# Two transformer blocks on one core: the first block's up-projections by seven products

## The chip, the cores and the metric

The kernel runs on one core of one Trainium2 chip. The metric is the time of one execution on the device in microseconds (us), as the median of several runs. The core has five engines that take instructions of their own queues in order: TensorE (PE in the rows, PEld for its weight loads), the vector engine VectorE (DVE), ScalarE (ACT), GpSimd (POOL) and SyncE (SP), which here mostly issues transfers. An instruction waits until what it needs has been signalled by the others.

## The reference

Two blocks of two layers each work on x, 512 tokens of 1024 features in fp32. What the change touches is the feed-forward step of the first block:

```
up = h2 @ w_up[l]                       # 1024 x 5632
a, v = up[..., :D_FF], up[..., D_FF:]   # D_FF = 2816
a = causal_depthwise_conv(a, conv_w[l], conv_b[l])   # width 3, over tokens
x = x + (jax.nn.gelu(a, approximate=False) * v) @ w_down[l]
```

with h2 the normed x. The second block's feed-forward step is `silu(g) * u` on the same sizes, without the convolution. In front of each stands the block's attention, and between the blocks a norm.

## The kernel before

Features lie on the 128 partitions and tokens along a row, so a tile of x is 128x512. Every fp32 product is three products of a split operand: a value is hi (rounded by ScalarE, L132) plus lo (the rest, by VectorE, L133), and `mm3` computes hi·hi, hi·lo and lo·hi. Weights come as raw tiles of 512 KB (128x1024 fp32; six buffers) on SyncE's queue, in an order that a plan fixes ahead; `_emit` splits the next one into one of four pairs of hi and lo buffers (`put`), and `pump` lets it do so once TensorE's work on an earlier one is issued. A raw buffer is loaded anew once its split has read it. All engines work through their instructions in the order in which the program issues them.

The feed-forward step (`ffn`) goes by groups of 128 of the 2816 columns, 22 in all, in four parts: 6, 6, 4 and 6 groups (`FPARTS`). A part computes the up-projection of its groups, two at a time (a pair), then the down-projection: units of two groups by 512 output columns ("fd", 24 matmuls of 512 columns each), which add to x (L660). Behind the first such unit stands what is left of the part's last pair, and behind a part of four groups also the first product of the next part (`started`).

A pair is computed in one of two ways; `PLAIN` gives for each block the group from which the second is used. Plain: `pair` for "fa" and "fv", 96 matmuls of 512 columns; then ScalarE and VectorE do the convolution of a (L1081 to L1083), ScalarE the Gelu (L1084), VectorE the product with v (L1152) and the split of the result (L237, L238: acth and actl). By seven products (`spair`): the 1024 x 256 weights of a pair and the activations are halved both ways into 2x2 blocks, and seven products of sums of blocks (24 matmuls of 256 columns each) take the place of eight. Products of the same sum of activations need sums of weight blocks, which VectorE makes (L327, `sum0`, `sum1`, `sum2`, `post5`: four for each pair); the sums of activations are made once for each layer (`factors`). The parts of a result are put together from three accumulators A, D and B by copies on ScalarE (s1, p5, d) and steps on VectorE (L1110 to L1125). Before, the first block has PLAIN 22 (all plain) and the second 6 (groups 6 to 21, so eight pairs in each layer: three, two and three in the last three parts).

In the first block the memory of the later cross attention is normed in the background (`mem_norm`, `mem_split`) while the second layer's feed-forward step runs.

Of the kernel before, what the change touches and what calls it, by code (L numbers as in the profile page):

```python
# [4 lines left out]
F32 = mybir.dt.float32  # L5
# [5 lines left out]
MUL, ADD, SUB, MAX = ALU.mult, ALU.add, ALU.subtract, ALU.max  # L11
P = 128
S = 512
D = 1024
# [300 lines left out]
    return chunk(name, raws, [unit(r["kc"], nc_, split, (i,)) for i, r in enumerate(raws)])  # L315


def schunks(name, w, c1, c2):


    b = [block(w, r, 4, c, 256) for r, c in ((0, c1), (0, c2), (512, c2), (512, c1))]

    b11, b12, b22, b21 = b
    box = {}

    def add(c, to, x, y):
        c.nc.vector.tensor_tensor(to, x, y, op=ADD)  # L327

    def sum0(c, r):

        box["t"] = c.pf.tile([P, 1024], F32, tag="t0", bufs=1, name=c.nm("t0")).rearrange("p (k c) -> p k c", k=4)
        add(c, box["t"], r[0], r[1])

    def sum1(c, r):

        add(c, r[0], r[0], r[1])

    def sum2(c, r):

        add(c, r[0], r[0], r[1])  # L340

    def post5(c, r):

        add(c, r[0], r[0], r[1])

    def temp(c, hi, lo, raws):
        c.put(hi, lo, box.pop("t"))


    u = [dict(unit(4, 256, whole, (b11,), 0), pre=sum0, praws=(b11, b12)),  # L350
         dict(unit(4, 256, temp, (b11,), 0), pre=sum1, praws=(b12, b22)),
         dict(unit(4, 256, whole, (b11,), 0), pre=sum2, praws=(b11, b12)),
         unit(4, 256, whole, (b22,), 1),
         dict(unit(4, 256, whole, (b21, b11), 1, 1), post=post5, praws=(b21, b11)),
         unit(4, 256, whole, (b12,), 1),
         unit(4, 256, whole, (b21,), 1)]
    out = [chunk(name, [], [x]) for x in u]
    out[0]["raws"] = b
    return out
# [77 lines left out]
FPARTS = ((0, 6), (6, 12), (12, 16), (16, 22))  # L437
FPARTS_END = ((0, 6), (6, 12), (12, 18), (18, 22))

PLAIN = (22, 6)  # L440


def ffn_plan(wu, wd, b, end=False):
    pl, late, first = [], [], []
    pairs = {f: schunks("fs", wu, 2816 + 128 * f, 128 * f) for f in range(PLAIN[b], 22, 2)}
    parts = FPARTS_END if end else FPARTS
    for f0, f1 in parts:
        for f in range(f0, f1, 2):
            if f < PLAIN[b]:
                pl.append(wchunk("fa", wu, 0, 8, 128 * f))  # L450
                pl.append(wchunk("fv", wu, 0, 8, 2816 + 128 * f))
                continue

            c = pairs[f]
            if not first:
                pl += c[:1] + late
            pl += c[1:6]
            late, first = c[6:], []
        if end and f1 == 22:
            pl += late  # L460
            for i in range(4):
                pl.append(wchunk("fd", wd, 128 * f0, f1 - f0, 256 * i))
            continue
        for i in range(2):
            for f in range(f0, f1, 2):
                pl.append(chunk("fd", [block(wd, 128 * f, 2, 512 * i, 512)], [unit(2, 512)]))
                if i == 0 and f == f0:
                    pl += late
                    late = []
                    if f1 - f0 == 4 and f1 >= PLAIN[b]:  # L470
                        first = pairs[f1][:1]
                        pl += first
    return pl


class Kern(Ctx):
# [515 lines left out]
                yield  # L992


    def factors(self):


        nc = self.nc
# [18 lines left out]
        for j in range(5):  # L1017
            cur = None
            if j < 4:
                xa, xb = self.t("xa"), self.t("xb")  # L1020
                for t, k in ((xa, j), (xb, j + 4)):
                    nc.vector.scalar_tensor_tensor(t, self.x[k], self.ngain(k), self.Rb, op0=MUL, op1=MUL)
                a11, a21, a12, a22 = xa[:, H[0]], xa[:, H[1]], xb[:, H[0]], xb[:, H[1]]
                s14, s23 = self.t("s14"), self.t("s23")
                tt(s14[:, H[0]], a22, a21, op=SUB)
                tt(s23[:, H[0]], a11, s14[:, H[0]], op=ADD)
                tt(s23[:, H[1]], a21, a11, op=SUB)
                tt(s14[:, H[1]], s23[:, H[0]], a12, op=SUB)
                cur = a11, xb, s14, s23
                yield  # L1030
            if last:
                a11, xb, s14, s23 = last
                if j % 2:
                    two = self.ft("Ah"), self.ft("Al")
                put(a11, ("11",), tiles=two, at=256 * ((j - 1) % 2))
                put(s14, ("1", "4"))
                put(s23, ("2", "3"), scale=-1.0)
                rest.append(xb)
            last = cur
            yield  # L1040
# [28 lines left out]
    def ffn(self, l, after, conv):  # L1069
# [22 lines left out]
        def spair(f, ah, al):  # L1092

            A, D, B = (self.ps() for _ in range(3))
            half = lambda t, nt: t[:, H[nt]]
            self.product(A, "11", True)
            yield
            s1 = self.t("s1")
            nc.scalar.copy(s1, A)
            self.product(D, "1", True)  # L1100
            self.settle()
            p5 = self.t("p5")
            nc.scalar.copy(p5, D)
            self.product(A, "2", False)
            a = [self.t("a") for _ in range(2)]
            self.product(D, "4", False)
            d = self.t("d")
            nc.scalar.copy(d, D)
            for nt in range(2):
                nc.vector.scalar_tensor_tensor(a[nt][:, H[0]], half(A, nt), -1.0, half(d, nt), op0=MUL, op1=SUB)  # L1110
            self.finish(gf)
# [27 lines left out]
        for i, (f0, f1) in enumerate(parts):  # L1139
            end = f1 == 22  # L1140
            ah, al = lists[i]
            for f in range(f0, f1, 2):
                if f < plain:
# [12 lines left out]
                    if f == 0:  # L1156
                        self.first_pair(self.next("fa"), ev_a, self.norm_gen())
                        if plain < 22:
                            gf = self.bg(self.factors())
                    else:  # L1160
                        self.pair("fa", ev_a)
                    self.pair("fv", ev_v)
# [17 lines left out]
            for c in range(2):  # L1180
# [18 lines left out]
                for u in range(0, n, 2):  # L1199
# [12 lines left out]
                    if u == 0 and c == 0:  # L1212
                        if last is not None:

                            end_of(last)
                            last = None
                        if end:
                            after[0]()
                            self.A = None
                        if n == 4 and f1 >= plain:  # L1220
                            started = spair(f1, *lists[i + 1])
                            next(started)
                        self.settle()


    def mem_norm(self):
# [16 lines left out]
        nc.vector.tensor_copy(self.mr, r)  # L1243
        self.mRb = self.pc.tile([P, 256], F32, tag="mRb", name="mRb")
        nc.scalar.copy(self.mRb, ps)
        yield from self.mem_split(0, mem)

    def mem_load(self):
# [755 lines left out]
    def program(self):  # L2004
# [17 lines left out]
        for l in range(2):  # L2022
# [2 lines left out]
                nc.gpsimd.dma_start(self.bias, self.a["bias"])  # L2025
                self.mixer1(l)
            if l == 0:
                self.ffn(0, (lambda: self.norm_begin(lambda j: self.pcol("norm1", 8 + j)), True, None), conv=True)
        with tc.tile_pool(name="vk", bufs=1) as self.pk:
            with tc.tile_pool(name="vm", bufs=1) as self.pv:  # L2030
                self.nbig = 1
                gm = self.bg(self.mem_norm())
                self.ffn(1, (lambda: self.norm_begin(lambda j: self.gfm[:, j:j + 1], lambda j: self.pcol("norm_f", j)), True, None), conv=True)
                self.finish(gm)
            with tc.tile_pool(name="v2", bufs=1) as self.pv:
                self.even()
# [86 lines left out]
```

## Time and profile before

| | us |
|---|---|
| median of 3 runs | 2723.52 (2722.99 to 2723.58) |
| profiled execution | 2723.18 |
| its span | 2721.5 |
| TensorE busy | 2685.9 (99%) |
| VectorE busy | 1636.9 (60%) |
| ScalarE busy | 1098.1 (40%) |
| GpSimd busy | 278.4 (10%) |

The span runs from the first to the last instruction that the profile has. Busy time is an average over all stages; what an engine has to spare in one stage is read from the table by stretch. In a timeline a row is one instruction (or xN in a row) with its start, its duration and, in brackets, how long its engine stood idle ahead of it and what ended that. Matmuls overlap, so their spacing is taken from start to start. The granted clock (PEclk) is the share of TensorE's full clock that the chip allowed.

### The profile page before, as it was taken

What the parts mean: (1) busy time and instruction counts of PE and PEld (TensorE: products, weight loads), DVE (VectorE), ACT (ScalarE), POOL (GpSimd) and SP (SyncE); (2) the same over time, 40 slices, a digit from 0 to 9 for tenths busy, and PEclk for the clock granted to TensorE, in tenths of its full rate; (3) what the DMA queues carried; (4) which work ended last, traced back from release to release, by engine and by line L of the source; (5) the groups of instructions that cost most, each with busy time, mean ns of one, the idle gap of its engine ahead of it and who ended that gap; (6) DMA issues with size and microseconds to landing.
All of it is one profiled execution on the core that took longest, in us unless ns stands there. A gap on an engine that the chain in (4) does not pass through costs nothing.

```text
span 2721.5 us, 36076 instructions
## 1 busy us (share of the span) xinstructions
PE 2685.9 (99%) x14462; PEld 2294.9 (84%) x14462; DVE 1636.9 (60%) x2418; ACT 1098.1 (40%) x1656; POOL 278.4 (10%) x345
## 2 busy tenths in 40 slices
PE   8999999999999999999999999999999999999997
PEld 7888888888878888888878888899988888889997
DVE  5644654455455375554556667776766656677766
ACT  4353332333345334332342354443443535534334
POOL 2110200001011011110031101000011001100001
PEclk9999999999999999999999999999999999999999
DMA  5232323322322223323323333243233113223231
GB/s 192 62 94 75 96 93 93 108 94 89 112 78 76 80 86 105 108 89 93 95 92 119 96 100 96 86 125 99 81 103 87 51 52 104 83 93 117 86 101 55
DMA packets 236423, 254.76 MB, mean 94 GB/s; under 512 B 19904, under 2 KB 212672, under 8 KB 235616
## 3 DMA queue, kind: packets, MB, share of 16 engines
q1 hardware_dynamic: 233808, 245.70, 29.5%
q0 software_dynamic: 1440, 5.97, 0.7%
q8 instruction: 113, 1.85, 0.3%
q10 hardware_dynamic: 1008, 0.80, 0.1%
q14 instruction: 54, 0.44, 0.1%
HBM read 248.20 MB, written 2.10 MB: 92 GB/s over the span
## 4 chain that ended last, share of the span: by engine, by line
PE 94%; DVE 3%; ACT 2%; issue 1%; POOL 0%; DMA 0%; ACTq 0%; POOLq 0%; SPq 0%; DVEq 0%
PE ps L225 25%; PE ps L227 25%; PE ps L226 25%; PE ps L1065 12%; PE ps L964 1%; PE ps L1740 1%; PE ps L800 1%; DVE lo L133 1%; PE ps L575 1%; PE ps L1466 1%; PE ps L979 0%; PE ps L890 0%; PE ps L584 0%; ACT hi L132 0%; PE ps L1875 0%
## 5 line engine op out<-in xcount | busy, mean ns | idle before, releaser
L133 DVE TENSOR_TENSOR lo<-raw,hi 128x1024 fp32r<-128x1024 f32 (+2 forms) x515 | 606.6, 1204 | 257.6 <-ACT hi L132 254.8
L225 PE MATMUL ps<-xh,hi 128*128 128x512 f32 x1712 | 673.2, 393 | 8.2 <-ACT hi L132 8.2
L227 PE MATMUL ps<-xh,lo 128*128 128x512 f32 x1712 | 667.4, 390 | 0.7 <-DVE lo L133 0.7
L226 PE MATMUL ps<-xl,hi 128*128 128x512 f32 x1712 | 667.1, 390 | 0.0
L132 ACT ACTIVATE hi<-raw 128x1024 fp32r<-128x1024 f32 (+2 forms) x515 | 505.1, 1013 | 293.5 <-PE ps L226 229.1
L225 PEld LDWEIGHTS ps<-xh,hi 128*128 128x128 f32 x1712 | 321.9, 188 | 76.1 <-ACT hi L132 8.2
L227 PEld LDWEIGHTS ps<-xh,lo 128*128 128x128 f32 x1712 | 321.7, 188 | 69.5 <-DVE lo L133 1.9
L226 PEld LDWEIGHTS ps<-xl,hi 128*128 128x128 f32 x1712 | 322.0, 188 | 65.2 <-issue 0.2
L225 PE MATMUL ps<-acth,hi 128*128 128x512 f32 (+1 forms) x736 | 280.8, 382 | 2.2 <-ACT acth L237 2.2
L226 PE MATMUL ps<-actl,hi 128*128 128x512 f32 (+1 forms) x736 | 280.7, 381 | 0.6 <-DVE actl L238 0.6
L227 PE MATMUL ps<-acth,lo 128*128 128x512 f32 (+1 forms) x736 | 280.1, 381 | 0.0
L1065 PE MATMUL ps<-Ah,hi 128*128 128x256 f32 x896 | 254.6, 284 | 0.9 <-DVE a L1116 0.9
L1065 PE MATMUL ps<-Al,hi 128*128 128x256 f32 x896 | 253.5, 283 | 0.0
L1065 PE MATMUL ps<-Ah,lo 128*128 128x256 f32 x896 | 253.5, 283 | 0.0
L660 DVE TENSOR_TENSOR x<-ps,x 128x512 f32<-128x512 f32 x168 | 114.8, 688 | 158.7 <-PE ps L227 158.4
L1065 PEld LDWEIGHTS ps<-Ah,hi 128*128 128x128 f32 x896 | 171.8, 192 | 2.6 <-issue 1.1
L1065 PEld LDWEIGHTS ps<-Al,hi 128*128 128x128 f32 x896 | 171.9, 192 | 0.4
L1065 PEld LDWEIGHTS ps<-Ah,lo 128*128 128x128 f32 x896 | 171.9, 192 | 0.0
L225 PEld LDWEIGHTS ps<-acth,hi 128*128 128x128 f32 x736 | 138.8, 189 | 28.7 <-ACT acth L237 2.6
L226 PEld LDWEIGHTS ps<-actl,hi 128*128 128x128 f32 x736 | 138.8, 189 | 27.1 <-DVE actl L238 1.3
L227 PEld LDWEIGHTS ps<-acth,lo 128*128 128x128 f32 x736 | 138.8, 189 | 26.4
L541 POOL TENSOR_TENSOR sq<-sq,sq 128x512 f32<-128x512 f32 (+1 forms) x57 | 76.5, 1349 | 661.5 <-ACT sq L535 661.0
(400 smaller groups left out, 3788.3 us busy)
## 6 DMA issues: line engine op xcount, KB each, us to landing
raw<-in_w_up SPq DMA_DIRECT2D x88, 512.0 KB, 3.7
raw<-in_ffn_w_gate_up SPq DMA_DIRECT2D x88, 512.0 KB, 3.6
raw<-in_w_in SPq DMA_DIRECT2D x78, 512.0 KB, 4.5
raw<-in_w_down SPq DMA_DIRECT2D x44, 512.0 KB, 4.4
raw<-in_ffn_w_down SPq DMA_DIRECT2D x44, 512.0 KB, 3.8
raw<-in_od_w_in SPq DMA_DIRECT2D x20, 512.0 KB, 3.8
raw<-in_w_o SPq DMA_DIRECT2D x16, 512.0 KB, 3.6
raw<-in_xattn_wkv SPq DMA_DIRECT2D x16, 512.0 KB, 4.5
```

Source lines behind the costliest of these rows:

```text
L132: self.nc.scalar.activation(hi, raw, AF.Copy)
L133: self.nc.vector.tensor_tensor(lo, raw, hi.bitcast(F32), op=SUB)
L225: mm(out, lhsT=wh, rhs=xh, start=first, stop=False)
L226: mm(out, lhsT=wh, rhs=xl, start=False, stop=False)
L227: mm(out, lhsT=wl, rhs=xh, start=False, stop=last)
L541: (nc.vector if dve else nc.gpsimd).tensor_tensor(acc[to], acc[to], q, op=ADD)
L575: nc.tensor.matmul(ps[:, i:i + 1], lhsT=q[:, t], rhs=self.ones[:, 0:1], start=(b == 0), stop=(b == len(sq) - 1))
L660: self.nc.vector.tensor_tensor(self.x[j], ps, self.x[j], op=ADD)
L800: nc.tensor.matmul(z[b][:, o:o + n], lhsT=k[rs, kt * P:(kt + 1) * P], rhs=q[rs, kt * P:S], start=(kt != 3), stop=False, skip_group_check=True)
L964: nc.tensor.matmul(o, lhsT=v, rhs=pt, start=not started[hh], stop=False, skip_group_check=True)
L1065: mm(o, lhsT=w, rhs=x, start=(first and nt == 0 and j == 0 and i == 0), stop=(j == 3 and i == 2), skip_group_check=True)
L1466: nc.tensor.matmul(p, lhsT=self.xv[:, kb, h * P:(h + 1) * P], rhs=pt[kb], start=(kb == 0), stop=(kb == 1))
```

## The change

`PLAIN` becomes (6, 6): the first block, too, computes groups 6 to 21 of each layer by seven products, 16 pairs in the two layers. For these the products come in another order than in the second block: "1", "11", "4", "2", "12", "3" and, behind the next pair's first, "22". VectorE makes two sums for each pair (t = W11 + W12, later t = t + W22), and two more are made by transfers of GpSimd's queue that add to what stands in their target: W22 from DRAM onto the raw tile of W12 (L335 of the changed kernel), and the raw tile of W21 onto t (L361). t has two buffers. The convolution and the Gelu follow in `act_a` as before, on the two results of L1154. The first part of each layer makes the sums of the activations in finer steps (`slow`), and the memory's split waits until the last part's first down-projection unit (`tail`). Lines from L319 on are numbered anew: in the changed kernel the sums are L327, the copies L1123, a's first half L1148, the sum of s1 L1151, a's second half L1154, the convolution L1106 to L1109, the products with s1 and with v L1158 and L1163; L132, L133, L237 and L238 keep their numbers.

```diff
-def schunks(name, w, c1, c2):
+def schunks(name, w, c1, c2, dma):
...
     def sum0(c, r):
-        box["t"] = c.pf.tile([P, 1024], F32, tag="t0", bufs=1, name=c.nm("t0")).rearrange("p (k c) -> p k c", k=4)
+        box["t"] = c.pf.tile([P, 1024], F32, tag="t0", bufs=1 + dma, name=c.nm("t0")).rearrange("p (k c) -> p k c", k=4)
         add(c, box["t"], r[0], r[1])
+        if dma:
+            c.nc.gpsimd.dma_start(r[1], b22["dma"][0][1], accum_op=ADD)
...
+    def temp_kept(c, hi, lo, raws):
+        c.put(hi, lo, box["t"])
+    def sum3(c, r):
+        add(c, box["t"], box["t"], r[0])
+    def sum4(c, r):
+        c.nc.gpsimd.dma_start(box["t"], r[0], accum_op=ADD)
+    if dma:
+        u = [dict(unit(4, 256, temp_kept, (b11,), 0), pre=sum0, praws=(b11, b12)),
+             unit(4, 256, whole, (b11,), 1),
+             dict(unit(4, 256, whole, (b22,), 0), pre=sum3, praws=(b22,)),
+             dict(unit(4, 256, temp_kept, (b21,), 0), post=sum4, praws=(b21,)),
+             unit(4, 256, whole, (b21,), 0),
+             unit(4, 256, whole, (b12, b22), 2),
+             unit(4, 256, temp, (b21,), 1)]
+    else:
...
-PLAIN = (22, 6)
+PLAIN = (6, 6)
...
+                if slow:
+                    yield
...
+            if conv:
+                self.product(D, "1", True)
+                yield
+                p5 = kept(D, "p5")
+                self.product(A, "11", True)
+                self.settle()
+                s1 = kept(A, "s1")
+                self.product(D, "4", False)
+                d = kept(D, "d")
+                a = [self.t("a") for _ in range(2)]
+                self.product(A, "2", False)
+            else:
...
                         if end:
                             after[0]()
                             self.A = None
+                            self.tail = True
...
         nc.scalar.copy(self.mRb, ps)
+        while not self.tail:
+            yield
         yield from self.mem_split(0, mem)
...
-                self.ffn(0, (lambda: self.norm_begin(lambda j: self.pcol("norm1", 8 + j)), True, None), conv=True)
+                with self.fpool(11):
+                    self.ffn(0, (lambda: self.norm_begin(lambda j: self.pcol("norm1", 8 + j)), True, None), conv=True)
```

What this does to VectorE's order is shown at two places of the first layer. In the names, lo and hi are split weights, raw their loaded tiles, t0 the sum t, a and y the halves of an activation, ps an accumulator. First the second pair of the second part (groups 8 and 9). VectorE before, from the first group's activation to the second's split:

```order
L1148 TENSOR_TENSOR a654_3868<-ps647_3831,Rb532_3095 128x512
L1082 SCALAR_TENSOR_TENSOR y655_3870<-a654_3868,prm_78,y655_3870 128x511
L1083 SCALAR_TENSOR_TENSOR y655_3870<-a654_3868,prm_78,y655_3870 128x510
L1148 TENSOR_TENSOR a657_3901<-ps656_3876,Rb532_3095 128x512
L1082 SCALAR_TENSOR_TENSOR y658_3903<-a657_3901,prm_78,y658_3903 128x511
L1083 SCALAR_TENSOR_TENSOR y658_3903<-a657_3901,prm_78,y658_3903 128x510
L133 TENSOR_TENSOR lo661_3935<-raw625_3670,hi660_3934 128x1024
L133 TENSOR_TENSOR lo663_3939<-raw629_3716,hi662_3938 128x1024
L1152 TENSOR_TENSOR y655_3870<-ps659_3909,y655_3870 128x512
L238 TENSOR_TENSOR actl667_3948<-y655_3870,acth666_3947 128x512
L1152 TENSOR_TENSOR y658_3903<-ps668_3951,y658_3903 128x512
L238 TENSOR_TENSOR actl670_3978<-y658_3903,acth669_3977 128x512
```

VectorE in the changed kernel, from the second sum ahead of the first pair's L1154 on:

```order
L327 TENSOR_TENSOR t0681_3882<-t0681_3882,raw667_3744 128x1024
L1154 SCALAR_TENSOR_TENSOR a685_3891<-ps670_3790,p5675_3822 128x256
L1154 SCALAR_TENSOR_TENSOR a686_3892<-ps670_3790,p5675_3822 128x256
L1107 SCALAR_TENSOR_TENSOR y695_3987<-a685_3891,prm_78,y695_3987 128x511
L1108 SCALAR_TENSOR_TENSOR y695_3987<-a685_3891,prm_78,y695_3987 128x510
L1107 SCALAR_TENSOR_TENSOR y696_3992<-a686_3892,prm_78,y696_3992 128x511
L1108 SCALAR_TENSOR_TENSOR y696_3992<-a686_3892,prm_78,y696_3992 128x510
L133 TENSOR_TENSOR lo701_4025<-raw667_3744,hi700_4024 128x1024
L1158 TENSOR_TENSOR y695_3987<-y695_3987,s1678_3852 128x256
L1158 TENSOR_TENSOR y696_3992<-y696_3992,s1678_3852 128x256
L133 TENSOR_TENSOR lo703_4055<-t0681_3882,hi702_4054 128x1024
L133 TENSOR_TENSOR lo706_4086<-raw682_3885,hi705_4085 128x1024
```

and the rest of the lap, up to the next L1154:

```order
L238 TENSOR_TENSOR actl708_4092<-y695_3987,acth707_4091 128x512
L238 TENSOR_TENSOR actl710_4096<-y696_3992,acth709_4095 128x512
L133 TENSOR_TENSOR lo713_4126<-raw650_3662,hi712_4125 128x1024
L327 TENSOR_TENSOR t0714_4129<-raw683_3887,raw691_3951 128x1024
L133 TENSOR_TENSOR lo721_4165<-t0714_4129,hi720_4164 128x1024
L1148 SCALAR_TENSOR_TENSOR a718_4138<-ps697_3997,d717_4136 128x256
L1148 SCALAR_TENSOR_TENSOR a719_4139<-ps697_3997,d717_4136 128x256
L133 TENSOR_TENSOR lo723_4195<-t0681_3882,hi722_4194 128x1024
L1151 TENSOR_TENSOR s1711_4099<-ps699_3999,s1711_4099 128x512
L133 TENSOR_TENSOR lo726_4226<-raw683_3887,hi725_4225 128x1024
L327 TENSOR_TENSOR t0714_4129<-t0714_4129,raw694_3983 128x1024
L1154 SCALAR_TENSOR_TENSOR a718_4138<-ps697_3997,p5704_4059 128x256
```

The two convolutions stand one behind the other ahead of the next weights' lo (lo701), and L1148, which reads the accumulator that product "3" takes next, stands behind the sum t0714 and its lo721. ScalarE in the changed kernel at the same place:

```order
L1106 ACTIVATE y695_3987<-a685_3891,prm_78 128x512
L1109 ACTIVATE y695_3987<-y695_3987 128x512
L1106 ACTIVATE y696_3992<-a686_3892,prm_78 128x512
L1109 ACTIVATE y696_3992<-y696_3992 128x512
L132 ACTIVATE hi700_4024<-raw667_3744 128x1024
L132 ACTIVATE hi702_4054<-t0681_3882 128x1024
L1123 COPY p5704_4059<-ps698_3998 128x512
L132 ACTIVATE hi705_4085<-raw682_3885 128x1024
```

The second half's y and both Gelus stand ahead of the split of the next weights (hi700).

The second place is the end of the part of four groups (groups 12 to 15), its last pair. VectorE before, from the second group's activation on:

```order
L1148 TENSOR_TENSOR a755_4547<-ps754_4522,Rb532_3095 128x512
L1082 SCALAR_TENSOR_TENSOR y756_4549<-a755_4547,prm_78,y756_4549 128x511
L1083 SCALAR_TENSOR_TENSOR y756_4549<-a755_4547,prm_78,y756_4549 128x510
L133 TENSOR_TENSOR lo759_4581<-raw723_4316,hi758_4580 128x1024
L133 TENSOR_TENSOR lo761_4585<-raw727_4362,hi760_4584 128x1024
L1152 TENSOR_TENSOR y753_4516<-ps757_4555,y753_4516 128x512
L238 TENSOR_TENSOR actl765_4594<-y753_4516,acth764_4593 128x512
L1152 TENSOR_TENSOR y756_4549<-ps766_4597,y756_4549 128x512
L238 TENSOR_TENSOR actl768_4624<-y756_4549,acth767_4623 128x512
```

and in the changed kernel, from the second half's convolution on:

```order
L1107 SCALAR_TENSOR_TENSOR y854_5175<-a843_5073,prm_78,y854_5175 128x511
L1108 SCALAR_TENSOR_TENSOR y854_5175<-a843_5073,prm_78,y854_5175 128x510
L133 TENSOR_TENSOR lo860_5197<-raw846_5102,hi859_5196 128x1024
L1158 TENSOR_TENSOR y853_5170<-y853_5170,s1836_5036 128x256
L1158 TENSOR_TENSOR y854_5175<-y854_5175,s1836_5036 128x256
L133 TENSOR_TENSOR lo863_5241<-raw850_5137,hi862_5240 128x1024
L133 TENSOR_TENSOR lo869_5274<-raw861_5200,hi868_5273 128x1024
L1163 TENSOR_TENSOR y853_5170<-ps822_4934,y853_5170 128x256
L1163 TENSOR_TENSOR y854_5175<-ps822_4934,y854_5175 128x256
L238 TENSOR_TENSOR actl872_5282<-y853_5170,acth871_5281 128x512
```

Three lo (lo860, lo863, lo869) now stand between the convolution and the result's split, and of these lo869 is of w_down weights whose raw tile is loaded after lo860.

## Rows read from the trace of the kernel before

**Rows 1.** The page, part 4: the chain that ended last, shares of the span.

```profile
PE 94%; DVE 3%; ACT 2%; issue 1%; POOL 0%; DMA 0%; ACTq 0%; POOLq 0%; SPq 0%; DVEq 0%
```

**Rows 2.** Timeline of TensorE: start, duration, engine, line, operation, what ended idle time.

```profile
1700.00 0.39 PE L225 MATMUL ps<-xh,hi 128*128 128x512 f32 x1
...
1704.08 0.39 PE L225 MATMUL ps<-xh,hi 128*128 128x512 f32 x1
...
1760.87 0.28 PE L1065 MATMUL ps<-Ah,hi 128*128 128x256 f32 x1
...
1763.03 0.28 PE L1065 MATMUL ps<-Ah,hi 128*128 128x256 f32 x1
```

**Rows 3.** By stretch, second block: length, busy PE, PEld, DVE, ACT, POOL; PEclk, DMA share, GB/s.

```profile
1776.00:1797.00 21.00, 21.00 (x176) 20.90 (x175) 17.84 (x24) 10.83 (x15) 0.00 (x0) 1.00 0.36 104
...
1665.00:1760.00 95.00, 94.97 (x426) 78.39 (x426) 74.07 (x112) 37.55 (x53) 8.91 (x7) 1.00 0.27 87
```

**Rows 4.** Timelines of VectorE, then ScalarE: convolution of a plain pair, first block.

```profile
577.43 0.69 DVE L1148 TENSOR_TENSOR a<-ps,Rb 128x512 f32<-128x512 f32 x1 [0.67 <-PE ps L227]
579.01 0.75 DVE L1082 SCALAR_TENSOR_TENSOR y<-a,prm,y 128x511 f32<-128x511 f32 x1 [0.89 <-ACT y L1081]
579.80 0.75 DVE L1083 SCALAR_TENSOR_TENSOR y<-a,prm,y 128x510 f32<-128x510 f32 x1
...
587.70 1.48 DVE L133 TENSOR_TENSOR lo<-raw,hi 128x1024 fp32r<-128x1024 f32 x1 [1.71 <-ACT hi L132]
...
578.16 0.82 ACT L1081 ACTIVATE y<-a,prm 128x512 f32<-128x512 f32 x1 [2.84 <-DVE a L1148]
580.64 0.63 ACT L1084 ACTIVATE y<-y 128x512 f32<-128x512 f32 x1 [1.66 <-DVE y L1083]
...
586.08 0.63 ACT L1084 ACTIVATE y<-y 128x512 f32<-128x512 f32 x1 [1.67 <-DVE y L1083]
586.62 1.05 ACT L132 ACTIVATE hi<-raw 128x1024 fp32r<-128x1024 f32 x1
```

**Rows 5.** Timeline of VectorE, second block: one pair, from L1116 to the next.

```profile
1778.95 0.42 DVE L1116 SCALAR_TENSOR_TENSOR a<-ps,p 128x256 f32<-128x256 f32 x1
1781.54 1.23 DVE L133 TENSOR_TENSOR lo<-raw,hi 128x1024 fp32r<-128x1024 f32 x1 [1.84 <-ACT hi L132]
1782.68 0.42 DVE L1120 TENSOR_TENSOR a<-a,s 128x256 f32<-128x256 f32 x1
1783.35 1.22 DVE L133 TENSOR_TENSOR lo<-raw,hi 128x1024 fp32r<-128x1024 f32 x1
...
1788.35 1.29 DVE L238 TENSOR_TENSOR actl<-a,acth 128x512 fp32r<-128x512 f32 x2 [0.43 <-ACT acth L237]
1790.30 1.23 DVE L133 TENSOR_TENSOR lo<-raw,hi 128x1024 fp32r<-128x1024 f32 x1 [0.66 <-ACT hi L132]
1791.44 1.22 DVE L327 TENSOR_TENSOR t<-raw,raw 128x1024 f32<-128x1024 f32 x1
...
1799.52 0.42 DVE L1116 SCALAR_TENSOR_TENSOR a<-ps,p 128x256 f32<-128x256 f32 x1
```

**Rows 6.** Timeline of TensorE, second block: first products after the part of four groups.

```profile
1904.59 0.50 PE L225 MATMUL ps<-acth,hi 128*128 128x512 f32 x1 [1.66 <-ACT acth L237]
...
1905.66 0.40 PE L227 MATMUL ps<-acth,lo 128*128 128x512 f32 x1
...
1909.77 0.40 PE L226 MATMUL ps<-actl,hi 128*128 128x512 f32 x1
```

**Rows 7.** By stretch, just behind that wait; PEclk is the value 0.50.

```profile
1906.00:1909.00 3.00, 3.00 (x9) 2.35 (x8) 1.70 (x2) 0.01 (x1) 0.00 (x0) 0.50 0.03 5
```

**Rows 8.** DMA issues: tiles, queue, operation, count, KB each, median us to landing.

```profile
raw<-in_w_down SPq DMA_DIRECT2D x44, 512.0 KB, 4.4
...
bias<-in_bias POOLq DMA_DIRECT2D x2, 1024.0 KB, 6.1
```

More of the change, by code (lines that the diff above doesn't have):

```diff
@@ L347, in temp @@
         c.put(hi, lo, box.pop("t"))
[L350 to L356, printed above, removed]
+    def temp_kept(c, hi, lo, raws):
[13 more added lines that the diff above has]
+    else:
+        u = [dict(unit(4, 256, whole, (b11,), 0), pre=sum0, praws=(b11, b12)),
+             dict(unit(4, 256, temp, (b11,), 0), pre=sum1, praws=(b12, b22)),
+             dict(unit(4, 256, whole, (b11,), 0), pre=sum2, praws=(b11, b12)),
+             unit(4, 256, whole, (b22,), 1),
+             dict(unit(4, 256, whole, (b21, b11), 1, 1), post=post5, praws=(b21, b11)),
+             unit(4, 256, whole, (b12,), 1),
+             unit(4, 256, whole, (b21,), 1)]
     out = [chunk(name, [], [x]) for x in u]
@@ L438 @@
 FPARTS_END = ((0, 6), (6, 12), (12, 18), (18, 22))
-PLAIN = (22, 6)
+PLAIN = (6, 6)
 def ffn_plan(wu, wd, b, end=False):
     pl, late, first = [], [], []
-    pairs = {f: schunks("fs", wu, 2816 + 128 * f, 128 * f) for f in range(PLAIN[b], 22, 2)}
+    pairs = {f: schunks("fs", wu, 2816 + 128 * f, 128 * f, b == 0) for f in range(PLAIN[b], 22, 2)}
     parts = FPARTS_END if end else FPARTS
@@ L992, in mixer_a, with factors @@
                 yield
-    def factors(self):
+    def factors(self, slow):
         nc = self.nc
@@ L1095, in spair, with kept @@
             half = lambda t, nt: t[:, H[nt]]
[L1096 to L1108, printed above, removed]
+            def kept(ps, name):
+                t = self.t(name)
+                nc.scalar.copy(t, ps)
+                return t
+            if conv:
[10 more added lines that the diff above has]
+            else:
+                self.product(A, "11", True)
+                yield
+                s1 = kept(A, "s1")
+                self.product(D, "1", True)
+                self.settle()
+                p5 = kept(D, "p5")
+                self.product(A, "2", False)
+                a = [self.t("a") for _ in range(2)]
+                self.product(D, "4", False)
+                d = kept(D, "d")
             for nt in range(2):
@@ L1158, in ffn @@
                         if plain < 22:
-                            gf = self.bg(self.factors())
+                            gf = self.bg(self.factors(conv))
                     else:
@@ L1245, in mem_norm @@
         nc.scalar.copy(self.mRb, ps)
+        while not self.tail:
+            yield
         yield from self.mem_split(0, mem)
@@ L2032, in program @@
                 gm = self.bg(self.mem_norm())
-                self.ffn(1, (lambda: self.norm_begin(lambda j: self.gfm[:, j:j + 1], lambda j: self.pcol("norm_f", j)), True, None), conv=True)
+                self.tail = False
+                with self.fpool(5):
+                    self.ffn(1, (lambda: self.norm_begin(lambda j: self.gfm[:, j:j + 1], lambda j: self.pcol("norm_f", j)), True, None), conv=True)
                 self.finish(gm)
```

## The prediction

> **What bounds the kernel now.** I read the chain of work that ended last first: TensorE is 94% of it [rows 1], so a change pays by what it takes from TensorE, and costs whatever makes TensorE wait. Next TensorE's own list, for the spacing of matmuls: from 1700.00 to 1704.08 stand 18 products of 512 columns, 0.2267 us each; from 1760.87 to 1763.03 stand 18 of 256 columns, 0.120 each [rows 2]. Then the second block, which already runs the seven products. There the vector engine (VectorE) works 17.84 us of 21 [rows 3], and its list shows one pair after the other: the step L1116 comes at 1778.95 and again at 1799.52, a lap of 20.57 us [rows 5]. So in that stage two engines run neck and neck, and the question of this case is whether the first block, where each pair also has a convolution on the same engines, still fits.
>
> **What the change takes away.** A plain pair of up-projection columns is 96 matmuls of 512 columns, 96 x 0.2267 = 21.76 us. Seven products are 7 x 24 = 168 of 256 columns, 168 x 0.120 = 20.16 us (2.88 each). That is 1.60 us per pair; 8 pairs in each of two layers, so 12.8 per layer and 25.6 us in all [rows 2].
>
> **What a lap costs on VectorE and ScalarE now.** The order of the changed kernel puts these in a row after a pair's last but one product, with L1154 as zero. First the activation chain, from the plain pair's rows [rows 4]: L1154's first half and the hand-over 0.46 (0.42 for a 256-column operation, and 578.16 less the end of 577.43); ScalarE's y to L1107 0.85 (578.16 to 579.01); L1107 0.79; L1108 to the Gelu 0.84 (579.80 to 580.64); Gelu 0.54 (586.08 to 586.62); then the second y, which stands behind that Gelu on ScalarE, 0.85, 0.79 and 0.84 again; Gelu, split and hand-over to the lo of the next weights 1.62 (586.08 to 587.70). Sum 7.6 us, in which VectorE does some 4 us of work. In the second block the same stretch, L1116 to lo, is 2.59 (1778.95 to 1781.54) [rows 5]. From there by the same rows: lo 1.14 (8.7 so far), L1158 twice 0.67, two lo 2.28, L1163 twice 0.67, wait and two splits up to the next lo 0.43 + 1.95, lo 1.14 (15.9), sum 1.14, wait for the split of that very sum on ScalarE about 1.1, its lo 1.14, L1148 twice 0.67 (19.9), lo 1.14, L1151 0.60 (half of the 1.29 for two at 1788.35, less overlap), lo 1.14, second sum 1.14. The lap is **23.95 us against TensorE's 20.16**. Taken instead as a difference from the second block it is 20.57 + 5.0 for the longer chain - 2 x 1.14 for two sums fewer + 1.1 for the wait on the sum = 24.4, which is the other end.
>
> **Where TensorE meets that lap.** T is the start of the next pair's first product; L1154 follows "3", which ends at T, and is 0.6 late behind the second sum. (1) lo of "4" is ready at 0.6 + 7.6 + 1.2 = 9.4; TensorE wants it with the third matmul of "4", at 3 x 2.88 + 0.24 = 8.9: waits 0.5. (2) "3" overwrites the accumulator that L1148 reads; L1148 ends at 0.6 + 19.9 = 20.5, "3" is due at 6 x 2.88 + 0.5 = 17.8: waits 2.7. (3) One pair later L1154 is 1.1 late against TensorE, and "4" waits 1.0. (4) The third pair of a part prepares no sum for a successor (2.2 less): 1.1 + 17.7 = 18.8 against 18.3, 0.5. So a part of three pairs waits 4.7, in lumps of 2.7 at most. The first pair of a part has no lap ahead of it, and the down-projection behind gives VectorE time to catch up. The part of four columns groups (two pairs) waits 0.5 and, by (2) without the sum, 0.5; then comes its second down-projection unit. Before it VectorE has, in order, the chain and lo (9.4 with the 0.6), a lo whose weights are loaded only when that lo has freed their buffer (4.4 us for w_down [rows 8]), hi 1.08, lo 1.14, L1163 0.42, split 0.6: 17.1 us. TensorE has one unit of 5.44 (24 x 0.2267) and two products meanwhile, 11.2: waits 5.9. The second block shows this very wait with the short chain: TensorE stands 1.66 us at 1904.59 for acth [rows 6]. Per layer 4.7 + 4.7 + 0.5 + 0.5 + 5.9 = 16.3 us.
>
> **The clock.** After that wait the granted clock was 0.50, so 1.2 in place of 2.4 GHz, from 1906 to 1909 [rows 7]; from 1905.66 to 1909.77 eleven matmuls took 4.11 us where 11 x 0.2267 = 2.49 do: 1.6 lost [rows 6]. I count it for the three waits over 2 us in each layer, 4.8; if none fell it would be 0, if each of the 1.0 waits too 8.
>
> **What costs nothing, and what covers it.** The three copies per pair on ScalarE stand in its gaps of the lap. The factors of the activations (half a dozen 256- to 512-column steps for each of four column groups) are now made in the first part of each layer too; in the second block this puts VectorE at 74.07 of 95 us with TensorE at 94.97 [rows 3], so 0, and up to 1.5 per layer if the slower convolution there shares badly. The memory's split now waits for the last part's down-projection: eight steps that VectorE does with 4 us; its cover there is TensorE's own unit, 0 to 2. **The transfers that add.** None is in the trace. The one that makes W21 - t (L361) is issued at 11.7 of the lap and read at some 18 by ScalarE: 6.3 us. Rows: 4.4 for a plain 512 KB load, 6.1 for 1024 KB through the GpSimd queue [rows 8]; it reads both sides, so I take 6.1 as nearest, which just fits. At twice that, 12.2, it would lengthen every lap with a successor by some 5 us; at 4.4 nothing changes, since the sum's own split is in front of it. The other (L335) has about a whole lap and costs 0 either way. The Trainium skill ("DMA: Bandwidth & Descriptors", Anatomy of one DMA) fits a GpSimd-issued transfer as 2.0 us plus bytes over 436e3, 3.2 us as an estimate for 512 KB. By that the slow transfer of rival three would have no chance; the row for 1024 KB is 6.1, where the fit has 4.4, so I keep a small one.
>
> **The sum.** Per layer -12.8 + 16.3 + 4.8 = +8.3, two layers +16.6, less rounding of the half-microsecond waits: 16. The profiled execution took 2723.18 us (its span 2721.5, 1.7 around it), 0.3 below the median of 2723.52, so they count as one: 2723.2 + 16 = **2739 us**.
>
> **The rivals.**
> - *The lap is absorbed.* Four split buffers hold 4 x 2.88 = 11.5 us of work for TensorE, and two laps only lose 2 x 3.8 = 7.6; if that lead is spent ahead of every wait, only the part of four groups stops, as in the second block [rows 6]. For it: the second block's lap is as long as TensorE's there and still TensorE is fed. Against it: (2) is a wait for an accumulator, which no lead in weights helps. Time: 2723.2 - 25.6 + 2 x (1.9 + 1.6) + some 2 = 2706.6; without any wait 2697.6. Chance 0.22.
> - *Half of it.* VectorE and ScalarE hand over sooner than the rows say, and half of the waits goes: per layer -12.8 + 8.2 + 4.8 = +0.2, so within 5.4 us of before, 2718 to 2728. Chance 0.16.
> - *The adding transfer is slow* (L361 over 6.3 us decides): at 12.2 us, 10 laps with a successor lose about 5 more each, to some 2780. For it: it moves three streams and none was seen. Against: the DMA engines' share is 0.36 [rows 3]. Chance 0.06.
> - *The forecast*, 2729 to 2752: the low end has no clock loss and the chain 0.5 shorter, the high end the lap of 24.4 (0.5 at each of ten waits) and clock losses of 8 a layer. Chance 0.56.
>
> A measurement of this kernel tells about 0.2%, 5.4 us, from no change. Faster 0.22 (rival one), same 0.16 (rival two), slower 0.62 (forecast and rival three). For 8 in 10 the range leaves out 0.11 below (the better half of rival one, with all waits gone) and 0.09 above: 2706 to 2752. The likeliest case alone is 2729 to 2752.
>
> **What would show it.** Right: in the first block's parts of three pairs TensorE stands about 2.7 us ahead of "3" of the second pair, ended by L1148 on VectorE; VectorE's L1154 comes every 23.4 us or more; TensorE waits 4 to 6 us for acth in the part of four groups, in both layers; the granted clock falls behind each. Wrong: laps of 20.2 with TensorE unbroken (rival one: the waits of ScalarE for VectorE were hidden), or ScalarE's hi from t waiting for a transfer of over 6.3 us (rival three). The matmul sum is wrong if 168 products take other than 20.16 us.

## The result and the profile after

The changed kernel takes 2758.97 us (median of 4 runs, 2757.54 to 2759.85) against 2723.45 for the kernel before beside it: ratio 1.0131, 95% interval 1.0116 to 1.0146. It is slower, as forecast, but by 35.5 us where 16 were forecast, and the time lies outside the range, which ended at 2752. The profiled execution took 2757.54 us, its span 2755.1.

The chain that ended last (part 4 of the page of after), and from the list of transfers those of GpSimd's queue that add (count, KB each, median us to landing); to be set beside [rows 1] and [rows 8].

```profile
PE 83%; DVE 8%; ACT 5%; issue 3%; DMA 0%; POOL 0%; ACTq 0%; DVEq 0%; POOLq 0%; SPq 0%
...
raw<-in_w_up POOLq DMA_DIRECT2D x16, 512.0 KB, 6.0
...
t<-raw POOLq DMA_DIRECT2D x16, 512.0 KB, 4.6
```

TensorE falls from 94% of the chain to 83%: VectorE and ScalarE have come into it. The two adding transfers land in 6.0 and 4.6 us.

Where the time went is read by stage, from the last step on x (L660 before, L683 after) of one part to that of the next, in us:

| part of the feed-forward step, first block | before | after | difference |
|---|---|---|---|
| layer 0: plain part | 100.5 | 100.5 | 0.0 |
| three pairs | 97.9 | 100.0 | +2.1 |
| two pairs (and the next part's first product) | 65.3 | 75.0 | +9.7 |
| three pairs | 99.3 | 98.5 | -0.8 |
| layer 1: plain part | 101.4 | 108.3 | +6.9 |
| three pairs | 97.9 | 99.9 | +2.0 |
| two pairs | 65.3 | 75.8 | +10.5 |
| three pairs | 103.3 | 106.8 | +3.5 |

The sum is +33.9, the spans differ by 33.6; the stages outside these agree within 0.3 us, but for the stretch ahead of the first part, which is 0.65 shorter. The part of two pairs now holds the first product of the next part (24 x 0.120 = 2.9 us), which the last part is therefore without. TensorE's own time in the three parts would be 93.1, 65.0 and 91.6 us (before, less 1.60 for each pair, and 2.9 moved), so in layer 0 they are too long by 6.9, 10.0 and 6.9. It is two different things: the pairs, which cost 11 to 12 us in each layer instead of gaining 12.8, and 11 us more in layer 1 alone, at the plain part and at the end.

**Inside the pairs.** The second part of layer 0, TensorE in the second and third pair:

```profile
478.33 0.39 PE L1090 MATMUL ps<-Ah,hi 128*128 128x256 f32 x1 [0.80 <-ACT p L1123]
...
483.11 0.39 PE L1090 MATMUL ps<-Ah,hi 128*128 128x256 f32 x1 [1.64 <-ACT s L1123]
...
489.63 0.36 PE L1090 MATMUL ps<-Ah,hi 128*128 128x256 f32 x1 [0.52 <-DVE a L1148]
...
502.38 0.38 PE L1090 MATMUL ps<-Ah,hi 128*128 128x256 f32 x1 [1.01 <-ACT p L1123]
...
507.15 0.39 PE L1090 MATMUL ps<-Ah,hi 128*128 128x256 f32 x1 [1.64 <-ACT s L1123]
```

Five waits; from start to start of the matmuls they cost 0.96, 1.80, 0.68, 1.17 and 1.80 us, 6.4 together (the brackets leave out the fill of the first matmul), and the part's whole excess over 0.2267 and 0.120 us per matmul is 6.9 (the rest is a slightly wider spacing right behind a wait). Four of them end with a copy on ScalarE that empties the accumulator which the next product overwrites. VectorE at the same place, one lap:

```profile
469.35 0.75 DVE L1154 SCALAR_TENSOR_TENSOR a<-ps,p 128x256 f32<-128x256 f32 x2
...
476.90 1.23 DVE L133 TENSOR_TENSOR lo<-raw,hi 128x1024 fp32r<-128x1024 f32 x1 [1.71 <-ACT hi L132]
...
488.74 0.75 DVE L1148 SCALAR_TENSOR_TENSOR a<-ps,d 128x256 f32<-128x256 f32 x2
...
493.40 0.75 DVE L1154 SCALAR_TENSOR_TENSOR a<-ps,p 128x256 f32<-128x256 f32 x2
```

L1154 to the next weights' lo takes 7.55 us (7.6 in the prediction), the lap 24.05 (23.95); the next lap, which prepares no sum, takes 22.69 (to 516.09). No idle time of VectorE in the first was ended by TensorE. And ScalarE there:

```profile
475.82 1.04 ACT L132 ACTIVATE hi<-raw 128x1024 fp32r<-128x1024 f32 x1
476.77 1.04 ACT L132 ACTIVATE hi<-t 128x1024 fp32r<-128x1024 f32 x1
477.72 0.56 ACT L1123 COPY p<-ps 128x512 f32<-128x512 f32 x1
...
481.44 1.15 ACT L237 ACTIVATE acth<-y 128x512 fp32r<-128x512 f32 x2 [2.20 <-DVE y L1163]
482.49 0.56 ACT L1123 COPY s<-ps 128x512 f32<-128x512 f32 x1
```

The copy of p5 stands behind two splits that came late behind the Gelus; the copy of s1 behind the splits of the result, which wait for VectorE's L1163. This is where the late lap reaches TensorE first.

**The part of four groups.** TensorE's second down-projection unit, and ScalarE's split of its neighbour:

```profile
607.88 0.80 PE L225 MATMUL ps<-acth,hi 128*128 128x512 f32 x1 [4.67 <-ACT acth L237]
...
604.51 1.06 ACT L132 ACTIVATE hi<-raw 128x1024 fp32r<-128x1024 f32 x1 [4.01 <-DMA raw<-in_w_down]
```

The wait is 4.7 us (4.8 from start to start; 5.9 forecast), in layer 1 4.9, for the reason forecast: a lo of w_down stands ahead of L1163 on VectorE, and ScalarE has stood 4.0 us for the raw tile before it could make the hi. Behind it the granted clock fell to 0.50 (1.2 GHz), which cost 2.2 us up to 612.1; behind the waits of 0.80 and 1.64 at 478 and 483 it stayed at 1.00:

```profile
478.00:483.00 5.00, 3.13 (x24) 2.93 (x24) 4.63 (x9) 2.80 (x6) 0.88 (x1) 1.00 0.64 163
483.00:488.50 5.50, 5.39 (x45) 5.39 (x46) 3.66 (x4) 3.49 (x5) 1.29 (x1) 1.00 0.66 178
609.00:612.00 3.00, 3.00 (x8) 2.32 (x8) 1.01 (x3) 0.29 (x1) 0.00 (x0) 0.50 0.31 109
```

(busy time by stretch, columns as in [rows 3]).

**Layer 1.** At the end of the plain part, where the memory's norm is finished in the background, and at the end of the layer, where the first products of the memory follow, TensorE:

```profile
1144.28 1.01 PE L607 MATMUL ps<-cst,ry 128*128 128x128 f32 x4 [3.60 <-DVE ry L587]
...
1450.26 0.58 PE L225 MATMUL ps<-memh,hi 128*128 128x256 f32 x1 [3.88 <-ACT hi L132]
...
1451.94 0.58 PE L227 MATMUL ps<-memh,lo 128*128 128x256 f32 x1 [0.88 <-DVE lo L133]
```

Before, the same small products did not wait, and behind both waits the clock fell too (TensorE before, then two stretches after):

```profile
1128.74 0.61 PE L584 MATMUL ps<-cst,ry 128*128 128x128 f32 x4
...
1144.90:1148.00 3.10, 3.10 (x9) 2.50 (x9) 3.10 (x5) 2.68 (x6) 0.00 (x0) 0.51 0.06 6
1450.00:1454.00 4.00, 2.85 (x11) 2.56 (x12) 3.76 (x2) 1.16 (x2) 3.01 (x2) 0.50 0.22 61
```

The first waits for the 12 small steps of the memory's rsqrt, which VectorE reaches late (1141.90 to 1144.06), 6.5 us later in the part than before. In its order the sums of activations that the change adds to this part stand ahead of them; no run took these away, so that they are the reason is read from the order. The second waits for the first weights' split, which ScalarE and VectorE reach late behind the memory's split (L1302, L1303): the change has moved that into the last part, where the next norm also runs.

### The profile page after: what moved, and what is told of

Its sections match the earlier page's. It is cut to its first block, busy times and chain, and to the rows that moved or that the text cites. A ratio compares the mean times of both kernels' runs of the same rounds, so it can differ in the third digit from the quotient of the medians.

```text
span 2755.1 us, 38874 instructions
## 1 busy us (share of the span) xinstructions
PE 2675.9 (97%) x15614; PEld 2335.8 (85%) x15614; DVE 1777.7 (65%) x2658; ACT 1181.9 (43%) x1784; POOL 273.0 (10%) x345
## 4 chain that ended last, share of the span: by engine, by line
PE 83%; DVE 8%; ACT 5%; issue 3%; DMA 0%; POOL 0%; ACTq 0%; DVEq 0%; POOLq 0%; SPq 0%
PE ps L225 20%; PE ps L226 20%; PE ps L227 20%; PE ps L1090 16%; DVE lo L133 2%; ACT hi L132 2%; PE ps L987 1%; DVE y L1107 1%; ACT y L1106 1%; DVE y L1108 1%; DVE t L327 1%; PE ps L1781 1%; PE ps L823 1%; ACT acth L237 1%; PE ps L1507 0%
## 5 line engine op out<-in xcount | busy, mean ns | idle before, releaser
L133 DVE TENSOR_TENSOR lo<-raw,hi 128x1024 fp32r<-128x1024 f32 (+2 forms) x515 | 605.7, 1197 | 266.7 <-ACT hi L132 263.7
L132 ACT ACTIVATE hi<-raw 128x1024 fp32r<-128x1024 f32 (+2 forms) x515 | 507.6, 1013 | 253.7 <-PE ps L226 147.4
L1090 PE MATMUL ps<-Ah,hi 128*128 128x256 f32 x1792 | 510.3, 285 | 28.7 <-ACT s L1123 16.4
L1090 PE MATMUL ps<-Ah,lo 128*128 128x256 f32 x1792 | 506.6, 283 | 0.0
L1090 PE MATMUL ps<-Al,hi 128*128 128x256 f32 x1792 | 506.3, 283 | 0.0
L225 PE MATMUL ps<-xh,hi 128*128 128x512 f32 x1200 | 474.2, 395 | 7.2 <-ACT hi L132 7.2
L227 PE MATMUL ps<-xh,lo 128*128 128x512 f32 x1200 | 468.7, 391 | 1.2 <-DVE lo L133 1.2
L226 PE MATMUL ps<-xl,hi 128*128 128x512 f32 x1200 | 468.2, 390 | 0.0
L1090 PEld LDWEIGHTS ps<-Ah,hi 128*128 128x128 f32 x1792 | 342.9, 191 | 35.5 <-ACT s L1123 18.5
L1090 PEld LDWEIGHTS ps<-Al,hi 128*128 128x128 f32 x1792 | 343.0, 191 | 0.9
L1090 PEld LDWEIGHTS ps<-Ah,lo 128*128 128x128 f32 x1792 | 342.6, 191 | 0.0
L227 PEld LDWEIGHTS ps<-xh,lo 128*128 128x128 f32 x1200 | 225.7, 188 | 50.3 <-DVE lo L133 2.9
L683 DVE TENSOR_TENSOR x<-ps,x 128x512 f32<-128x512 f32 x168 | 114.3, 688 | 128.4 <-PE ps L227 127.9
```

The source lines that it names most:

```text
L132: self.nc.scalar.activation(hi, raw, AF.Copy)
L133: self.nc.vector.tensor_tensor(lo, raw, hi.bitcast(F32), op=SUB)
L225: mm(out, lhsT=wh, rhs=xh, start=first, stop=False)
L226: mm(out, lhsT=wh, rhs=xl, start=False, stop=False)
L227: mm(out, lhsT=wl, rhs=xh, start=False, stop=last)
L683: self.nc.vector.tensor_tensor(self.x[j], ps, self.x[j], op=ADD)
```

## The experiments

All are edits of the changed kernel unless said; the code is shortened. Three theories stood at first. L: the lap of VectorE and ScalarE, 24.05 us against TensorE's 20.16, makes the waits, and where they show is a matter of order. Q: the copies' places in ScalarE's queue are the loss. T: the sums and the adding transfers make the waits. Times are medians; the kernel before ran beside them at 2722.5 to 2723.1.

**e1, without the convolution's two shifted columns in the pairs.**

```
-for nt in (0, 1): y = a * w2 + b ; y[1:] += a[:-1] * w1 ; y[2:] += a[:-2] * w0 ; gelu(y)
+for nt in (0, 1): y = a * w2 + b      # ScalarE; the two += were L1107 and L1108 on VectorE
+for nt in (0, 1): gelu(y)
```

> In the 16 new pairs the two steps of the convolution that add a's shifted columns (L1107, L1108) are left out, and both y stand ahead of the Gelus; the result is therefore not the reference's. Theory L (the lap of VectorE and ScalarE, 24.05 us measured against TensorE's 20.16, makes the waits): the chain from L1154 to the next weights' lo falls from 7.6 to about 3 us, the lap to about 19.5, the waits inside the pairs go (6.4 us in each part of three pairs, 2.8 in the part of four groups) and the wait for acth falls from 4.8 to under 2: about 2722 us in place of 2759. Rival T (the sums and the adding transfers make the waits): no change beyond 5 us, 2754 or more.

Measured 2713.88. The parts of three pairs in layer 0 fall to 93.3 and 91.9 us, which is TensorE's own time (93.1 and 91.6), and the part of two pairs to 67.3, with a wait of 1.6 for acth left. The sums and the transfers are still there, so theory T falls. The edit does two things: it takes the shifted columns from VectorE and puts both y ahead of the Gelus. The second alone gives 18 of the 45 us (e3); the other 27 are VectorE's work on the convolution, the load that makes the lap too long. It came out 8 us below what was expected; 5.5 of them are in the parts of two pairs, mostly since the clock no longer fell there behind the shorter wait.

**e2, the copies of the accumulators first.**

```
-self.product(D, "1", True); yield; p5 = kept(D, "p5")       # behind the next splits
+self.product(D, "1", True, then=copy p5)                    # ahead of them
-self.product(A, "11", True); self.settle(); s1 = kept(A, "s1")
+self.product(A, "11", True, then=copy s1); self.settle()
```

> The copies that free TensorE's accumulators are issued earlier on ScalarE: p5 right behind product 1, ahead of the splits of the next weights; s1 right behind product 11, ahead of the splits of the result. Theory Q (the copies stand in the wrong place of ScalarE's queue, and that is the whole loss): the waits of 0.96, 1.80, 1.17 and 1.80 us go, 14 us per layer: about 2731 us. Theory L: VectorE's lap stays at 24 us, and the waits come back one product later, ahead of 3, for L1148, as the prediction had them: 4.7 in place of 6.4 us per part of three pairs, about 1.5 less in the part of four groups, about 2749 us.

Measured 2754.50, so theory Q falls: 4.5 us gained, of the 28 that it would give. TensorE's waits in the same part are now

```profile
479.09 0.38 PE L1090 MATMUL ps<-Ah,lo 128*128 128x256 f32 x1 [0.75 <-DVE lo L133]
...
490.07 0.35 PE L1090 MATMUL ps<-Ah,hi 128*128 128x256 f32 x1 [2.33 <-DVE a L1150]
...
503.15 0.39 PE L1090 MATMUL ps<-Ah,lo 128*128 128x256 f32 x1 [0.75 <-DVE lo L133]
```

(L1150 is the former L1148). They cost 0.92, 2.49, 0.92 and 0.36, 4.7 us: the pattern of the prediction's steps (1) to (4), 0.5, 2.7, 1.0 and 0.5, and its sum. The prediction had left the copies out; with the copies out of the way its waits stand there. In the part of two pairs nothing was gained, since the wait for acth grew from 4.8 to 6.3 us.

**e3, both y ahead of the first Gelu.**

```
-for nt in (0, 1): y, L1107, L1108, Gelu
+for nt in (0, 1): y
+for nt in (0, 1): L1107, L1108
+for nt in (0, 1): Gelu
```

> Both y of the convolution are made on ScalarE ahead of the first Gelu, so that VectorE need not wait 1.47 us between the two halves. Theory L: the lap falls to 22.6 us, each lap with a successor gives TensorE 1.5 us back, the wait for acth too: some 9 us per layer, about 2741 us. If the lap does not set the waits: no change, 2759.

Measured 2740.70. VectorE's lap (L1170 is the former L1154):

```profile
469.53 0.75 DVE L1170 SCALAR_TENSOR_TENSOR a<-ps,p 128x256 f32<-128x256 f32 x2
...
492.08 0.75 DVE L1170 SCALAR_TENSOR_TENSOR a<-ps,p 128x256 f32<-128x256 f32 x2
```

It is 22.55 us, 22.6 expected. The gain from a change in the order of ScalarE alone is 18 us.

**e4, the memory's split not held back** (the two lines `while not self.tail: yield` are left out).

> The memory's split no longer waits for the last part; it runs right behind the memory's norm, as in the kernel before. If the late split makes the end of the second layer longer (TensorE stood 3.9 us ahead of the first product of the memory, and 0.9 behind it): 4 to 5 us less, about 2754. If something else does (the norm of x there): 2759.

Measured 2753.58. The last part of layer 1 goes from 106.8 to 102.0 us and no other part of a feed-forward step by more than 0.7: the late split is the cause of that one.

**e5, the result's product and splits earlier in the part of four groups.**

```
 end_of(last)            # product "22" of the part's last pair
 last = None
+if n == 4: self.settle()   # product with v, splits; now ahead of the next part's first product
```

> In the part of four groups (of both blocks) the product with v and the result's splits are issued right behind product 22, ahead of the next part's first product and of the lo that waits for a w_down load of 4 us. If that load is the cause of the 4.8 us wait for acth: VectorE reaches the product with v at 10.5 us of the chain in place of some 14.5, the wait falls to about 1 us (from 4.8 and 5.1 in the first block, 1.9 in the second) and the fall of the clock behind it goes: 2 x 5 us in the first block, 2 x 3.5 in the second, about 2742. If the length of the chain alone makes it: under 4 us gained, 2755 or more.

Measured 2741.75. The parts of two pairs go from 75.0 and 75.8 to 69.2 and 69.1, the one of the second block from 69.2 to 65.2. TensorE's wait there is left at

```profile
603.47 0.49 PE L225 MATMUL ps<-acth,hi 128*128 128x512 f32 x1 [0.46 <-ACT acth L237]
```

and the clock behind it no longer falls. The work in front of L1163, the 4 us of the load above all, is the cause; the length of the chain alone would have left 2755 or more.

**e6, the memory's norm spread** (three more `yield` between the rsqrt and the small products of L607; each lets a piece of other work be issued in between).

> Three more steps of other work are put between the memory's rsqrt (12 small steps of VectorE) and the small products on TensorE that need it, in the second layer's first part. If TensorE's 3.8 us wait there is only its place in the queue behind VectorE: 3 to 4 us less, about 2755. If VectorE is simply behind in that part because of the sums of activations: the wait shows elsewhere in the part, within 1 us of 2759.

Measured 2750.82. The plain part of layer 1 goes from 108.3 to 103.3 us, 5.0 less (the wait and the slower matmuls behind it), no other part of a feed-forward step by more than 0.8; the spans differ by 6.0. The rsqrt itself ends as late as without the edit (1144.30 against 1144.06), so it is TensorE's place behind it that cost. Of the 6.9 us there 1.9 are left, which only shows that they are not this wait.

**e7, the two transfers undone, VectorE makes all four sums.**

```
-gpsimd.dma_start(W12, W22, accum_op=ADD)    # L335
+vector: W12 = W12 + W22
-gpsimd.dma_start(t, W21, accum_op=ADD)      # L361
+vector: t = t + W21
```

> The two adding transfers are undone: VectorE adds W22 to W12 and W21 to t itself, at the places where the transfers were issued. Theory L: the lap grows by 2.3 us, each lap with a successor costs TensorE that, two laps in a part of three pairs and some 3.4 us in the part of four groups, 25 us in all: about 2784. Rival P (the transfers themselves cost, by their own time or on GpSimd's queue): no more than 15 us slower, or faster than 2759.

Measured 2782.36. L1154 comes at 468.84 and 494.71, a lap of 25.87: 1.8 us more for two sums of 1.14 (some of it was idle time). So the transfers save 23 us here; rival P, that they themselves cost, falls. Less than half of the 23 us is longer waiting: the waits of TensorE in the parts with pairs, from start to start, grow from 20.4 to 25.9 us in layer 0 and by 4.9 in layer 1. Most of the rest is slower matmuls: the clock fell inside the pairs behind the waits that had grown to 2.9 us:

```profile
509.73 0.58 PE L1090 MATMUL ps<-Ah,hi 128*128 128x256 f32 x1 [2.90 <-ACT s L1123]
...
509.80:512.00 2.20, 2.20 (x10) 2.20 (x11) 1.44 (x2) 2.20 (x3) 0.00 (x0) 0.50 0.40 154
```

So the 25 us that were expected came about in part by another way than the one expected.

**e8, all of it together, and the lap cut further.** Beside e3 to e6: p5's copy as in e2, s1's copy ahead of the result's splits but behind the next weights' split; the next weights' split issued between the y and the Gelus; L1148 ahead of the next lo.

```
 for y in ys: y = a * w2 + b ; L1107, L1108
+self.base += 1 ; self.pump(1)              # hi and lo of the next weights
 for y in ys: gelu(y)
...
-self.product(A, "2", False) ; L1148        # behind the lo that the product's pump issues
+self.product(A, "2", False, then=L1148)    # ahead of it
```

> All of it together with the lap cut further: both y first, the next weights' split issued between them and the Gelus, p5's and s1's copies ahead of ScalarE's queue, L1148 ahead of the next lo, the early product with v of e5, the spread norm of e6 and the memory's split as in e4. Theory L: the lap comes to about 20.3 us, as long as TensorE's, and the waits in the pairs and for acth go: 2723.2 - 25.6 for the products, - 7 for the second block's wait, + some 4 left in the second layer's first part, about 2695; within 2690 and 2705. If a bound not seen yet stands behind (loads, GpSimd's queue): 2710 or more.

Measured 2695.92. VectorE, the same place as above (L1178 is the former L1154, L1158 the former L1148):

```profile
470.66 0.75 DVE L1178 SCALAR_TENSOR_TENSOR a<-ps,p 128x256 f32<-128x256 f32 x2
...
474.86 1.22 DVE L133 TENSOR_TENSOR lo<-raw,hi 128x1024 fp32r<-128x1024 f32 x1
...
484.72 0.76 DVE L1158 SCALAR_TENSOR_TENSOR a<-ps,d 128x256 f32<-128x256 f32 x2 [0.29 <-PE ps L1090]
...
490.82 0.75 DVE L1178 SCALAR_TENSOR_TENSOR a<-ps,p 128x256 f32<-128x256 f32 x2
```

The lap is 20.16, TensorE's own, and it is now VectorE that waits for TensorE; TensorE has no wait left in the three parts of layer 0. The chain from L1154 to lo is 4.2 us, 3.3 shorter. The parts of layer 0 last 93.2, 65.0 and 91.7.

**e9, e10 and e11.** e9 is the kernel before with e5's two lines alone, e10 is e8 with e7's edit, e11 is e8 once more.

> The kernel before (first block plain), with only the early product with v and splits of e5 in the part of four groups, which acts in the second block alone. The waits there (1.9 us, the fall of the clock behind it and what follows) go in both layers: about 2715.5. So of e8's 27 us some 20 are from the seven products and their shorter lap in the first block. If the wait stays: 2722.5.

> e8 with both adding transfers undone: VectorE makes all four sums. Theory L: the lap goes from 20.2 (TensorE's own) to some 22.4 us and waits come back, about 4.5 us in a part of three pairs, 1 to 2 in the part of four groups: 2716. If in the shorter lap VectorE has room for two more sums: within 3 us of 2696.

> The kernel of e8 once more, for its interval: 2696, ratio about 0.990 to the kernel before, and about 0.993 to the kernel of e9.

Measured: e9 2719.63 (ratio to before 0.9990, interval 0.9980 to 0.9999); e10 2695.92; e11 2695.38 (ratio 0.9903, 0.9885 to 0.9921). e9 gained about 3 us where 7 were expected: only the first layer of the second block has a part of four groups in the middle, the last layer's parts are 6, 6, 6 and 4. So of the 27 us by which e8 beats the kernel before, about 24 (2719.63 - 2695.38) are the first block's seven products with the shorter lap and the mended places, of the 25.6 that the matmuls alone give.

e10 came out at e8's time, where the longer lap was expected to cost 20 us unless VectorE had room. Its lap is 22.0 us (22.4 expected), but only between the first two pairs of a part; the third follows after 18.5, since nothing is prepared for a fourth:

```profile
469.19 0.75 DVE L1178 SCALAR_TENSOR_TENSOR a<-ps,p 128x256 f32<-128x256 f32 x2
...
491.19 0.75 DVE L1178 SCALAR_TENSOR_TENSOR a<-ps,p 128x256 f32<-128x256 f32 x2
...
509.67 0.75 DVE L1178 SCALAR_TENSOR_TENSOR a<-ps,p 128x256 f32<-128x256 f32 x2
```

Of an excess of 1.8 us in one lap TensorE waits 0.43 from start to start; the rest is covered, it seems, by what VectorE is ahead of TensorE when a part begins. So the transfers are needed where the lap is 24 us long, and not where it is 20.

## Why the prediction was right in its sign and wrong in its size

The sign came out by the mechanism that was forecast, a lap of VectorE and ScalarE longer than TensorE's. The size failed at two steps. The larger is "What costs nothing": two terms put at 0 in the sum took 11.2 us. The other is "Where TensorE meets that lap", which left out the waits behind the copies on ScalarE.

- **The products.** 168 matmuls at 0.120 us, 20.16 for a pair: right; e1 and e8 show parts of three pairs at that time.
- **The lap.** 23.95 forecast, 24.05 measured, and what would show it (L1154 every 23.4 us or more) did in the laps that prepare a sum. Right, and shown to be the cause by e1, e3 and e8.
- **Where TensorE meets it.** Mis-sized. Step (1) gave 0.5 for the wait ahead of "4"; it is 0.96, and there are 1.80 more ahead of "2" that no step had, while the 2.7 of step (2) is 0.68: "the three copies per pair on ScalarE stand in its gaps of the lap" is the sentence that failed. A copy's time does fit, but it stands behind work that is late, and TensorE needs the accumulator that it empties. The waits are 6.4 in a part of three pairs where 4.7 were forecast. e2 shows the forecast's four waits once the copies are moved. The excess of the pairs' three parts is 23.8 us in layer 0, against 16.3 + 4.8 forecast: waits in the pairs 15.6 (10.4 forecast), the wait for acth 4.8 (5.9), the clock 2.2 (4.8), and 1.2 of wider spacing right behind the waits.
- **The wait for acth.** 5.9 forecast, 4.7 measured in layer 0 and 4.9 in layer 1, by the chain that was forecast (the w_down load, shown by e5).
- **The clock.** 1.6 us in each of three places of a layer were forecast; of these it fell in one, behind the longest wait. In the pairs of the parts of three it stayed at 1.00, also behind the 2.33 us of e2. It fell besides in two places that no term had, behind the two waits of layer 1 (0.51 and 0.50); their cost is in the 11.2 us below.
- **"What costs nothing."** The sums of activations were put at 0 to 1.5 us a layer and the memory's split at 0 to 2. In layer 0 the first was indeed 0.0; in layer 1 it met the memory's norm, +6.9 us, of which e6 takes back 5.0; the second is +3.5 in a part whose pairs behave as layer 0's did (-0.8), so 4.3, and e4 takes back 4.8. The cover named for the split, TensorE's own unit, did not help: what was late there is the split of the next weights, on the engines that the split itself loads. VectorE's load of 74 of 95 us in the second block's first part [rows 3] could not show it, because no memory is normed there.
- **The sum.** Forecast 2 x (-12.8 + 16.3 + 4.8) = 16.6. Measured, by the table, -25.6 + 23.8 + 24.5 (the parts with pairs) + 6.9 + 4.3 = 33.9. So of the 17.3 us between them 6.1 are the waits behind the copies and the wider spacing, less what the clock and acth cost below forecast, 11.2 the two places in layer 1. The range was too narrow at its top since each of these was held at its lower end there.
- **The rivals.** The absorbed lap (rival one) is what e8 reaches by another order, so it was no property of the buffers' lead. Half of it (rival two) did not occur: the lap was 24.05 where the rows gave 23.95, so the hand-overs were no shorter. The slow transfer (rival three) did not occur: 4.6 us where 6.3 were free, and where ScalarE waits ahead of a hi from t (486.50), it waits for VectorE's sum, not for the transfer. By its own terms it would have given 2739 + 10 x 5 = 2789, not 2780. The Trainium skill's fit ("DMA: Bandwidth & Descriptors", Anatomy of one DMA: 2.0 us plus bytes over 436e3, so 3.2 as an estimate) is below both adding transfers here, 4.6 and 6.0.

## What to carry to other kernels

Where a product form saves work on the matrix engine, add up the lap of the engines that feed it and empty it, in their own order and with their waits for each other, before counting the gain; if it is longer than the matrix engine's, the order of the work on these engines decides what it costs, and their shares of busy time do not show it (VectorE 65% after). Shorten it by order first: both halves' first steps ahead of either's last, the next weights' split into the wait, whatever frees an accumulator ahead of whatever waits for a load. And a background task that is moved is not covered by an engine that it does not run on: name who is queued behind it on its own engines.

## What was not expected of the hardware

The granted clock did not fall behind every wait of like length. It fell to 0.50 behind 1.66 us of waiting at 1904.59 of the kernel before [rows 6, 7] and, after, behind 4.67 at 607.88, 3.60 at 1144.28 (0.51) and 3.88 at 1450.26. It stayed at 1.00 behind 1.64 at 483.11 after and behind 2.33 at 490.07 in e2, where 256-column products came before and after the wait. Such products alone are not what kept it up: in e7 it fell to 0.50 behind 2.90 between them (509.73). What tells these apart was not tried. An adding transfer from one tile to another took 4.6 us, hardly more than the plain load of the same 512 KB (4.2 for w_down after, 4.4 before); the one from DRAM onto a tile 6.0.
